# The first block of a fused two-layer matmul: w1 in row pieces, x turned in float16, six banks filled side by side

## The chip, the cores and the metric

The kernel runs on one core of a Trainium2 chip. A core has TensorE (PE, matrix products and transposes into PSUM, which has eight banks), VectorE (DVE), ScalarE (ACT), GpSimd (POOL) and SyncE (SP); ScalarE, GpSimd and SyncE also issue the transfers (DMAs) used here. The metric is the time of one execution on the device in microseconds; lower is better.

## The reference

`x` is 16 x 512 x 768, so 8192 rows of 768; `w1` is 768 x 3072, `w2` is 3072 x 768, all float32.

```python
y = np.matmul(x, w1) + b1
y = np.maximum(y, 0)
return np.matmul(y, w2).astype(np.float32)
```

## The kernel before

The rows are cut into eight blocks of 1024 (`MB`), the 3072 hidden columns into two halves, so there are 16 iterations (`NIT`); iterations 0 to 7 take the first half of the hidden columns, 8 to 15 the second and add to what is in the output. In each iteration a first stage computes `relu(x w1 + b1)` for its block and a second multiplies by `w2`. All products are float16 with float32 sums in PSUM. From iteration 1 on both stages use a scheme with fewer products, made of sums of tiles (`X_SUMS`, `W1_SUMS`, `Y_SUMS`, `W2_SUMS`) that VectorE adds up. The first stage of iteration 0 is different: `first_block` (L1008) multiplies plainly, since the sums of w1 aren't there yet.

The order of the work is a plan: every step is a task of a `Graph` with an engine, an assumed duration, what it reads and writes, and sometimes a due time. TensorE's tasks run in the order in which they are added; for the other engines `Graph.run` simulates the plan and picks among ready tasks by due time. It also gives out PSUM banks (`take`), by the times at which the plan believes them free. `presets` (L729) holds the times at which the plan believes the first transfers to have landed. The plan only fixes the order on each engine and the banks: on the chip each instruction waits for what it needs, and each engine runs its instructions in order.

What happens ahead of and in the first block:

- `prologue` (L708): SyncE and ScalarE issue two tiles each of x (128 rows, float32, into the slots `self.s[0..3]`), ScalarE then the bias rows (`load_bias`, L676). GpSimd issues the first strip of w1 (`load_strip`: 256 columns, all 768 rows, 384 KB once cast to float16), makes the constants, and then issues two more strips, the second half of x's block (`load_x`, cast to float16 into `self.xn[4..7]`), three strips of the second column group, `w2`, and the next block's x. TensorE multiplies a tile of ones eight times meanwhile.
- `add_transpose_first(half, s)` (L908): a tile of 128 rows of x is turned on TensorE in two pieces of three 128 x 128 squares, each piece in a bank of its own; VectorE copies the first piece to `self.x`, ScalarE the second. The first half of the block (four tiles, `half` 0) is turned in float32, the second in float16.
- `add_plain(strip, j, m, parts, evict_parts, between)`: the product of 128 hidden columns with 512 rows of half `m`; with `parts` 2 in two runs of six products of 256 rows. `between` is added after the first run. ScalarE then evicts the bank with bias and relu (L990) into `self.y`.
- `add_bias` (L938): the bias rows are turned on TensorE, VectorE copies them (L946) and builds tables from them (L949 to L961).

`first_block` adds the four turns of x, then strips 0, 1, 2 for half 0 (the bias turn after the first run of six products), with the turns of the second half's tiles put between runs, then the rest. Two steps that stand on VectorE and ScalarE in the same stretch matter below: the sums of w1 (L842) and squares of the weights for a later range check (L874).

Of the kernel before, what the change touches and what calls it, by code (L numbers as in the profile page):

```python
# [10 lines left out]
FP16 = mybir.dt.float16  # L11
# [3 lines left out]
ACTF = mybir.ActivationFunctionType  # L15
# [3 lines left out]
P = 128  # L19
# [567 lines left out]
class Fast:  # L587
# [93 lines left out]
    def load_strip(self, to, c, g, h):  # L681
# [4 lines left out]
            out=to[:, g, 2 * h:2 * h + 2].rearrange("p a k h -> p (a k) h"),  # L686
            in_=w1r[:, :, h0:h0 + 2 * P])

    def load_w2(self, to, c, h, q):
        h0 = (12 * c + 4 * h + q) * P  # L690
        self.nc.gpsimd.dma_start(out=to[:, 2 * q:2 * q + 2, h, :],
                                 in_=self.w2[h0:h0 + P, :].rearrange("p (a n) -> p a n", a=2))
# [15 lines left out]
    def prologue(self):  # L708
        nc = self.nc
        for s in range(4):  # L710
            (nc.sync, nc.scalar)[s % 2].dma_start(out=self.s[:, s],
                                                  in_=self.xf[s * P:(s + 1) * P, :])
        self.load_bias()
        self.load_strip(self.v1, 0, 0, 0)
        self.constants()
        self.load_strip(self.v1, 0, 0, 1)
        self.load_strip(self.v1, 0, 0, 2)
        self.load_x(0, 1, 2)
        for h in range(3):
            self.load_strip(self.v1, 0, 1, h)  # L720
        for q in range(4):
            for h in range(3):
                self.load_w2(self.v2, 0, h, q)
        self.load_x(1, 0)
        for _ in range(8):
            nc.tensor.matmul(self.ps[:, 7, 0:P], lhsT=self.ones, rhs=self.ones, start=True,
                             stop=True)

    def presets(self):  # L729
        g = self.g  # L730
        for t, at in enumerate((9.3, 11.3, 13.3, 19.9, 21.8, 23.8)):
            for k in range(2):
                g.preset(("w1", t // 3, 2 * (t % 3) + k), at)
        for q in range(4):
            for h in range(3):
                for n in range(2):
                    g.preset(("w2", 2 * q + n, h), 24.8 + 3 * q + h)
        for s in range(4):
            g.preset(("xn", 4 + s), 15.2 if s < 2 else 17.2)
            g.preset(("xn", s), 39.5)  # L740
            g.preset(("rows", s), (5.3, 5.3, 7.2, 7.2)[s])
        g.preset("b1_rows", 5.0)
# [162 lines left out]

    def add_transpose_first(self, half, s):  # L908

        for a in range(2):  # L910
            ps = Reg("ps", leaves=0)

            def view(ps=ps):
                p = self.ps[:, ps.at[0], :]
                if half:
                    p = p[:, 0:3 * P // 2].bitcast(FP16)
                return p[:, 0:3 * P].rearrange("p (k m) -> p k m", k=3)

            def turn(a=a, view=view):
                ident = (self.ident, self.ident16)[half]  # L920
                rows = self.xn[:, 4 + s, :] if half else self.s[:, s]
                for k in range(3):
                    self.nc.tensor.transpose(view()[:, k, :],
                                             rows[:, (3 * a + k) * P:(3 * a + k + 1) * P], ident)

            def copy(a=a, view=view):
                out = self.x_part(4 * half + s)[:, 3 * a:3 * a + 3]
                if a:
                    self.nc.scalar.copy(out=out, in_=view())
                else:  # L930
                    self.nc.vector.tensor_copy(out=out, in_=view())  # L931
            r = 2 * half + s // 2
            self.g.add("PE", 210 if half else 380, turn, writes=[ps],
                       reads=[("xn", 4 + s)] if half else [("rows", s), self.hold[s]])
            self.g.add("ACT" if a else "DVE", 560, copy, reads=[ps],
                       writes=[("x", 2 * r + a, s % 2)])

    def add_bias(self):  # L938
        nc = self.nc
# [29 lines left out]
    def add_plain(self, strip, j, m, parts, evict_parts, between=None):  # L969
        gi, h = divmod(strip, 3)  # L970
        ps = Reg("ps", leaves=2 if parts == 1 else 0)
        nc = self.nc

        def product(n):
            cols = slice(n * self.QM, (n + 1) * self.QM) if parts == 2 else slice(0, 512)
            for k2 in range(2):
                for k in range(3):
                    a = 4 * m + k2
                    rhs = (self.x[:, a:a + 3:2, k, :] if parts == 1
                           else self.x[:, a + 2 * n, k, :])  # L980
                    nc.tensor.matmul(self.ps[:, ps.at[0], cols],  # L981
                                     lhsT=self.v1[:, gi, 2 * h + k2, k, j * P:(j + 1) * P],
                                     rhs=rhs, start=(k2 == 0 and k == 0),
                                     stop=(k2 == 1 and k == 2))

        def evict(a, b):
            n = 4 * h + 2 * gi + j
            i = 8 * m + 2 * gi + j
            out = self.y[:, i:i + 5:4, h * self.QM:(h + 1) * self.QM]
            nc.scalar.activation(out=out[:, a:b],  # L990
                                 in_=self.ps[:, ps.at[0], :].rearrange("p (a m) -> p a m",
                                                                       a=2)[:, a:b],
                                 func=ACTF.Relu, bias=self.b1y[:, n:n + 1])
        for n in range(parts):
            rows = (0, 1) if parts == 1 else (n,)
            nc = self.nc
            self.g.add("PE", 1300 // parts, lambda n=n: product(n),
                       reads=[("x", 4 * m + 2 * r + k2, q) for r in rows for k2 in range(2)
                              for q in range(2)] + [("w1", gi, 2 * h + k) for k in range(2)],
                       writes=[ps])  # L1000
            if n == 0 and between:
                between()
        for a, b in ((0, 2),) if evict_parts == 1 else ((0, 1), (1, 2)):
            self.g.add("ACT", 692 if evict_parts == 1 else 470, lambda a=a, b=b: evict(a, b),
                       reads=[ps, "b1y"],
                       writes=[("y", (2 * m + r) * 4 + 2 * gi + j, h) for r in range(a, b)])

    def first_block(self):  # L1008
        for s in range(4):
            self.add_transpose_first(0, s)  # L1010
        plain = self.add_plain
        for strip in range(3):
            for j in range(2):
                between = None
                if strip == 0 and j == 0:
                    between = self.add_bias
                elif strip == 2 and j == 1:
                    between = lambda: [self.add_transpose_first(1, s) for s in (0, 1)]
                plain(strip, j, 0, 2, 2 if strip == 1 else 1, between)
        plain(0, 0, 1, 2, 1, lambda: [self.add_transpose_first(1, s) for s in (2, 3)])  # L1020
        plain(0, 1, 1, 2, 1)
        for strip in (1, 2):
            for j in range(2):
                plain(strip, j, 1, 2, 2 if strip == 1 else 1)
        for strip in (3, 4, 5):
            for m in range(2):
                for j in range(2):
                    plain(strip, j, m, 1, 1)
# [514 lines left out]
```

## Time and profile before

| | |
|---|---|
| median of 3 runs | 852.05 us (851.43 to 852.44) |
| profiled execution | 851.03 us, span 849.4 us |
| granted TensorE clock | 0.999 |
| busy: PE, DVE, ACT, POOL | 839.5, 736.5, 568.5, 166.5 us |
| first product of the first block (L981) | starts at 9.50 us |
| last TensorE row of the timeline | starts at 841.79 us, lasts 1.30 us |

The span is the time from the first to the last instruction; the profiled execution's own time is 1.6 us longer. A row of the timeline gives the start in us, the duration, engine, line and operation, the tile written and the tile read, how many instructions are merged in it, and in brackets how long the engine had been idle and what ended that. PEld is TensorE loading weights, which overlaps its products. A `q` behind an engine's name is its queue of transfers.

### The profile page before, as it was taken

How to read it: one execution, taken by the hardware profiler on the slowest of the kernel's cores; microseconds unless marked ns; L12 is line 12 of the kernel's file. 1: busy time of each engine (PE TensorE's matmuls, PEld its weight loads, DVE VectorE, ACT ScalarE, POOL GpSimd, SP SyncE). 2: the span in 40 equal slices, each digit the busy share in tenths (PEclk: the TensorE clock that was granted, in tenths of full speed). 3: DMA queues.
4: the chain of work that ended last, by engine and by line, in shares of the span. 5: the costliest groups of instructions: out<-in, count | busy, mean ns of one | idle time of the engine just before them, and what ended most of it. 6: DMA issues, size and time to landing. Idle time of an engine off the chain costs nothing.

```text
span 849.4 us, 16770 instructions
## 1 busy us (share of the span) xinstructions
PE 839.5 (99%) x6381; PEld 625.1 (74%) x6381; DVE 736.5 (87%) x1229; ACT 568.5 (67%) x1203; POOL 166.5 (20%) x181
## 2 busy tenths in 40 slices
PE   8999999999999999999999999999999999999997
PEld 7558778587786867768687686877868677686874
DVE  5898988969889697988999989698896979979787
ACT  5866967678686784946859477766657666456462
POOL 5210011102111020110031503224041230502301
PEclk9999999999999999999999999999999999999999
DMA  9996597969789496593894968979789797975937
GB/s 212 202 180 175 82 230 108 198 140 160 198 109 203 117 154 164 96 249 123 232 177 82 193 109 148 160 110 176 124 130 147 122 164 113 154 126 75 167 85 178
DMA packets 170968, 128.93 MB, mean 152 GB/s; under 512 B 93805, under 2 KB 169349, under 8 KB 170885
## 3 DMA queue, kind: packets, MB, share of 16 engines
q0 software_dynamic: 57104, 69.61, 53.3%
q1 hardware_dynamic: 113312, 57.23, 28.4%
q8 instruction: 50, 0.82, 0.4%
q10 hardware_dynamic: 468, 1.00, 0.3%
q14 instruction: 34, 0.27, 0.1%
HBM read 73.15 MB, written 69.60 MB: 168 GB/s over the span
## 4 chain that ended last, share of the span: by engine, by line


## 5 line engine op out<-in xcount | busy, mean ns | idle before, releaser
L1197 PE MATMUL ps<-v,y 128*128 128x384 f16 x2496 | 408.5, 326 | 0.5 <-ACT s L1208 0.5
L1071 PE MATMUL ps<-x,v 128*128 128x256 f16 x3600 | 395.6, 273 | 0.0
L1071 PEld LDWEIGHTS <-v 128*128 128x128 f16 x3600 | 352.0, 98 | 42.5
L1197 PEld LDWEIGHTS <-y 128*128 128x128 f16 x2496 | 244.0, 98 | 160.9 <-issue 1.0
L1208 ACT ACTIVATE s<-ps 128x384 f32<-128x384 f32 (+1 forms) x244 | 153.8, 643 | 137.4 <-PE ps L1197 136.3
L1044 DVE TENSOR_TENSOR y<-y 128x768 f16<-128x768 f16 (+1 forms) x384 | 219.0, 618 | 2.5
L1114 DVE CUSTOM_DVE_ANT_0 y<-ps,s 128x512 f16<-128x512 f32 x240 | 155.7, 685 | 54.2 <-ACT s L1111 41.9
L1250 POOL DMA_DIRECT2D out_dram<-s x79 | 95.2, 1467 | 166.7 <-ACT s L1208 112.7
L1111 ACT ACTIVATE s<-ps,bt 128x256 f32<-128x256 f32 x180 | 75.1, 469 | 63.2 <-PE ps L1071 57.4
L826 DVE TENSOR_TENSOR x<-x 128x768 f16<-128x768 f16 (+1 forms) x210 | 113.8, 578 | 1.4
L706 POOL DMA_DIRECT2D xn<-in_x_dram x30 | 25.1, 838 | 258.4 <-ACT xn L766 153.8
L1111 ACT ACTIVATE y<-ps,bt 128x256 f16<-128x256 f32 x180 | 69.6, 486 | 7.7 <-PE ps L1071 7.7
L1214 DVE TENSOR_TENSOR s<-ps,s 128x768 f32<-128x768 f32 x74 | 70.5, 952 | 1.7 <-PE ps L1197 0.9
L1208 ACT ACTIVATE ps<-ps 128x384 f32<-128x384 f32 (+1 forms) x144 | 68.1, 512 | 5.0 <-PE ps L1197 3.2
L1214 DVE TENSOR_TENSOR s<-s,ps 128x768 f32<-128x768 f32 x60 | 57.0, 950 | 2.8 <-PE ps L1197 0.5
L766 ACT ACTIVATE xn<-xn 128x768 f16<-128x768 f16 x64 | 53.5, 837 | 1.2 <-DMA x<-xn 1.2
L1253 POOL DMA_DIRECT2D out_dram<-s x16 | 18.9, 1184 | 108.6 <-ACT s L1208 97.3
L1111 ACT ACTIVATE ps<-ps,bt 128x256 f32<-128x256 f32 x60 | 26.7, 445 | 19.2 <-PE ps L1071 18.2
L1107 ACT ACTIVATE ps<-ps 128x512 f32<-128x512 f32 x60 | 35.3, 588 | 3.6 <-DVE y L1114 3.5
L1122 DVE TENSOR_TENSOR s<-s,ps 128x512 f32<-128x512 f32 x30 | 20.6, 687 | 17.8 <-PE ps L1071 17.8
L981 PE MATMUL ps<-x,v 128*128 128x256 f16 (+1 forms) x216 | 32.0, 308 | 0.7 <-DVE x L931 0.7
L1117 DVE SCALAR_TENSOR_TENSOR s<-ps,bt,s 128x256 f32<-128x256 f32 x60 | 26.1, 476 | 4.4 <-PE ps L1071 4.4
(59 smaller groups left out, 302.6 us busy)
## 6 DMA issues: line engine op xcount, KB each, us to landing
out_dram<-s POOLq DMA_DIRECT2D x95, 384.0 KB, 7.6
out_dram<-s SPq DMA_DIRECT2D x69, 384.0 KB, 4.6
xn<-in_x_dram POOLq DMA_DIRECT2D x28, 768.0 KB, 9.2
v<-in_w_dram POOLq DMA_DIRECT2D x6, 384.0 KB, 10.6
v<-in_w_dram POOLq DMA_DIRECT2D x12, 192.0 KB, 9.0
w1d<-in_w_dram POOLq DMA_DIRECT2D x6, 384.0 KB, 6.8
w2d<-in_w_dram POOLq DMA_DIRECT2D x12, 192.0 KB, 5.4
v<-w1d SPq DMA_DIRECT2D x12, 192.0 KB, 4.2
```

The lines of the kernel that those rows point to most:

```text
L766: self.nc.scalar.activation(out=self.xn[:, s, :], in_=self.xn[:, s, :], func=ACTF.Square, accum_out=self.stat[:, self.stat_at["x"] + i:][: ...
L826: self.nc.vector.tensor_tensor(out=self.two(x, out), in0=self.two(x, in0), in1=self.two(x, in1), op=ALU.add if sign > 0 else ALU.subtract)
L981: nc.tensor.matmul(self.ps[:, ps.at[0], cols], lhsT=self.v1[:, gi, 2 * h + k2, k, j * P:(j + 1) * P], rhs=rhs, start=(k2 == 0 and k == 0), ...
L1044: self.nc.vector.tensor_tensor(out=self.two(self.y, out), in0=self.two(self.y, in0), in1=self.two(self.y, in1), op=ALU.add if sign > 0 els ...
L1071: nc.tensor.matmul(self.ps[:, at, j * self.QM:(j + 1) * self.QM], lhsT=self.v1[:, gi, self.w1s[c][gi][FIRST_V[p]], k, j * P:(j + 1) * P], ...
L1107: nc.scalar.activation(out=out, in_=ps, scale=float(a), func=func if kind == "out" else ACTF.Copy)
L1111: nc.scalar.activation(out=out[:, j], in_=ps[:, j], func=func, scale=float(a), bias=beta(j))
L1114: nc.vector._custom_dve(TENSOR_ADD_SAT, out=out, in0=ps, in1=s, s0=F_MAX, s1=0.0)
L1197: nc.tensor.matmul(self.ps[:, bank[ch].at[j], 0:NH], lhsT=self.y[:, ys[SECOND_U[p]], m0:m0 + P], rhs=self.v2[:, slot[SECOND_V[p]], h, :], ...
L1208: nc.scalar.activation(out=out, in_=ps, func=ACTF.Copy, scale=float(a))
L1214: engine.tensor_tensor(out=out, in0=in0, in1=in1, op=ALU.add if a == b else ALU.subtract)
L1250: nc.gpsimd.dma_start(out=rows, in_=out, accum_op=ALU.add)
```

## The change

The three strips of w1 of column group 0 are loaded as six pieces instead (`load_part`): piece k holds rows 128k to 128k+127 of all three strips, 192 KB in float16. The plan's table of landing times has the six pieces.

The first half's four tiles of x are first cast to float16 (`add_casts`, first half of each tile on VectorE, second on ScalarE, into unused slots of `self.y`), and turned in float16. A tile is now turned as one task of six squares into one bank; VectorE and ScalarE each copy half of that bank.

`first_rows` replaces strips 0 to 2 of half 0: six banks, one for each pair of strip and 128 columns, are filled side by side. For each piece k and each half n of the 512 rows, six products are added, one per bank, so that a bank is complete only with the last piece. The order is piece 0 for the first 256 rows, the turns of tiles 2 and 3, piece 1 for the first 256 rows, pieces 0 and 1 for the second, and then pieces 2 to 5 for both; the turns of the second half's tiles stand before piece 5 and after it. The six evictions (`add_evict`, moved out of `add_plain`) come at the end.

The bias turn (`add_bias`) is now added right after the casts, ahead of all turns of x; before, it came after the first six products.

```diff
+    def load_part(self, g, k):
+        w1r = self.w1.rearrange("(k p) (h c) -> p k h c", p=P, c=4 * P)
+        self.nc.gpsimd.dma_start(out=self.v1[:, g, k // 3:6:2, k % 3, :],
+                                 in_=w1r[:, k, 0:3, 2 * g * P:2 * (g + 1) * P])
...
-        self.load_strip(self.v1, 0, 0, 0)
+        self.load_part(0, 0)
         self.constants()
-        self.load_strip(self.v1, 0, 0, 1)
-        self.load_strip(self.v1, 0, 0, 2)
+        for k in range(1, 6):
+            self.load_part(0, k)
...
+    def add_casts(self):
+        for s in range(4):
+            for a in range(2):
...
+                    out, rows = self.y[:, 16 + s, cols], self.s[:, s, cols]
+                    if a:
+                        self.nc.scalar.copy(out=out, in_=rows)
+                    else:
+                        self.nc.vector.tensor_copy(out=out, in_=rows)
...
+    def add_transpose_first(self, half, rows):
+        for s in rows:
             ps = Reg("ps", leaves=0)
...
+                tile = self.xn[:, 4 + s, :] if half else self.y[:, 16 + s, :]
+                for k in range(6):
+                    self.nc.tensor.transpose(view(k // 3)[:, k % 3, :],
+                                             tile[:, k * P:(k + 1) * P], self.ident16)
...
+            for a in range(2):
+                self.g.add("ACT" if a else "DVE", 480, lambda a=a, copy=copy: copy(a), reads=[ps],
+                           writes=[("x", 2 * r + a, s % 2)])
...
+    def first_rows(self):
+        banks = {(h, j): Reg("ps", leaves=0) for h in range(3) for j in range(2)}
...
+        for k, n in ((0, 0), (1, 0), (0, 1), (1, 1), *((k, n) for k in range(2, 6) for n in range(2))):
+            for h, j in banks:
+                self.g.add("PE", 109, lambda k=k, n=n, h=h, j=j: product(k, n, h, j),
+                           reads=[("x", 2 * n + k // 3, q) for q in range(2)] + [("part", k)],
+                           writes=[banks[h, j]])
+            if (k, n) == (0, 0):
+                self.add_transpose_first(0, (2, 3))
+            elif (k, n) == (4, 1):
+                self.add_transpose_first(1, (0, 1))
+        self.add_transpose_first(1, (2, 3))
+        for h, j in banks:
+            self.add_evict(h, j, 0, banks[h, j], 1)
...
     def first_block(self):
-        for s in range(4):
-            self.add_transpose_first(0, s)
...
+        self.add_casts()
+        self.add_bias()
+        self.add_transpose_first(0, (0, 1))
+        self.first_rows()
+        for j in range(2):
+            plain(0, j, 1, 2, 1)
```

The plan's entry for the bias rows stays as it was, `g.preset("b1_rows", 5.0)`.

More of the change, by code (lines that the diff above doesn't have):

```diff
@@ L730, in presets @@
         g = self.g
-        for t, at in enumerate((9.3, 11.3, 13.3, 19.9, 21.8, 23.8)):
+        parts = (8.2, 9.2, 10.2, 11.2, 12.3, 13.4)
+        for k in range(6):
+            g.preset(("part", k), parts[k])
+        for h, at in enumerate((19.9, 21.8, 23.8)):
             for k in range(2):
-                g.preset(("w1", t // 3, 2 * (t % 3) + k), at)
+                g.preset(("w1", 0, 2 * h + k), parts[3 * k + 2])
+                g.preset(("w1", 1, 2 * h + k), at)
         for q in range(4):
@@ L904, in add_stats, with cast @@
             add()
-    def add_transpose_first(self, half, s):
-        for a in range(2):
-            ps = Reg("ps", leaves=0)
[L913 to L926, printed above, removed]
+    def add_casts(self):
+        for s in range(4):
+            for a in range(2):
+                cols = slice(3 * a * P, 3 * (a + 1) * P)
+                def cast(s=s, cols=cols, a=a):
+                    out, rows = self.y[:, 16 + s, cols], self.s[:, s, cols]
[3 more added lines that the diff above has]
+                        self.nc.vector.tensor_copy(out=out, in_=rows)
+                self.g.add("ACT" if a else "DVE", 560 if a else 500, cast,
+                           reads=[("rows", s), self.hold[s]], writes=[("cast", s, a)], due=0.0)
@@ new lines, in add_transpose_first, with view, turn, copy @@
+    def add_transpose_first(self, half, rows):
+        for s in rows:
+            ps = Reg("ps", leaves=0)
+            def view(a, ps=ps):
+                p = self.ps[:, ps.at[0], 0:3 * P].bitcast(FP16)[:, 3 * a * P:3 * (a + 1) * P]
+                return p.rearrange("p (k m) -> p k m", k=3)
+            def turn(s=s, view=view):
+                tile = self.xn[:, 4 + s, :] if half else self.y[:, 16 + s, :]
+                for k in range(6):
+                    self.nc.tensor.transpose(view(k // 3)[:, k % 3, :],
+                                             tile[:, k * P:(k + 1) * P], self.ident16)
+            def copy(a, s=s, view=view):
@@ L927, in copy @@
                 out = self.x_part(4 * half + s)[:, 3 * a:3 * a + 3]
                 if a:
-                    self.nc.scalar.copy(out=out, in_=view())
+                    self.nc.scalar.copy(out=out, in_=view(a))
                 else:
-                    self.nc.vector.tensor_copy(out=out, in_=view())
+                    self.nc.vector.tensor_copy(out=out, in_=view(a))
             r = 2 * half + s // 2
-            self.g.add("PE", 210 if half else 380, turn, writes=[ps],
-                       reads=[("xn", 4 + s)] if half else [("rows", s), self.hold[s]])
@@ L935, in add_transpose_first @@
-            self.g.add("ACT" if a else "DVE", 560, copy, reads=[ps],
-                       writes=[("x", 2 * r + a, s % 2)])
+            self.g.add("PE", 420, turn, writes=[ps],
+                       reads=[("xn", 4 + s)] if half else [("cast", s, a) for a in range(2)])
+            for a in range(2):
+                self.g.add("ACT" if a else "DVE", 480, lambda a=a, copy=copy: copy(a), reads=[ps],
+                           writes=[("x", 2 * r + a, s % 2)])
     def add_bias(self):
@@ L984, in product @@
                                      stop=(k2 == 1 and k == 2))
[L986 to L993, printed above, removed]
         for n in range(parts):
@@ L1002, in add_plain, with add_evict, evict @@
                 between()
+        self.add_evict(strip, j, m, ps, evict_parts)
+    def add_evict(self, strip, j, m, ps, evict_parts):
+        gi, h = divmod(strip, 3)
+        nc = self.nc
+        def evict(a, b):
+            n = 4 * h + 2 * gi + j
+            i = 8 * m + 2 * gi + j
+            out = self.y[:, i:i + 5:4, h * self.QM:(h + 1) * self.QM]
+            nc.scalar.activation(out=out[:, a:b],
+                                 in_=self.ps[:, ps.at[0], :].rearrange("p (a m) -> p a m",
+                                                                       a=2)[:, a:b],
+                                 func=ACTF.Relu, bias=self.b1y[:, n:n + 1])
         for a, b in ((0, 2),) if evict_parts == 1 else ((0, 1), (1, 2)):
@@ L1006, in add_plain, with product @@
                        writes=[("y", (2 * m + r) * 4 + 2 * gi + j, h) for r in range(a, b)])
+    def first_rows(self):
+        nc = self.nc
+        banks = {(h, j): Reg("ps", leaves=0) for h in range(3) for j in range(2)}
+        def product(k, n, h, j):
+            nc.tensor.matmul(self.ps[:, banks[h, j].at[0], n * self.QM:(n + 1) * self.QM],
+                             lhsT=self.v1[:, 0, 2 * h + k // 3, k % 3, j * P:(j + 1) * P],
+                             rhs=self.x[:, 2 * n + k // 3, k % 3, :],
+                             start=(n == 0 and k == 0), stop=(k == 5), skip_group_check=True)
+        for k, n in ((0, 0), (1, 0), (0, 1), (1, 1), *((k, n) for k in range(2, 6) for n in range(2))):
[10 more added lines that the diff above has]
+            self.add_evict(h, j, 0, banks[h, j], 1)
     def first_block(self):
-        for s in range(4):
-            self.add_transpose_first(0, s)
         plain = self.add_plain
[L1012 to L1021, printed above, removed]
+        self.add_casts()
[4 more added lines that the diff above has]
+            plain(0, j, 1, 2, 1)
         for strip in (1, 2):
```

## The prediction

> **What bounds the kernel now.** I read the page first, then the order of time of TensorE in the first 24 us, then, for the same stretch, the queues, the groups by shape and the order of time of VectorE. The page:
>
> ```profile
> span 849.4 us, 16770 instructions
> PE 839.5 (99%) x6381; PEld 625.1 (74%) x6381; DVE 736.5 (87%) x1229; ACT 568.5 (67%) x1203; POOL 166.5 (20%) x181
> ...
> L1197 PE MATMUL ps<-v,y 128*128 128x384 f16 x2496 | 408.5, 326 | 0.5 <-ACT s L1208 0.5
> ...
> L981 PE MATMUL ps<-x,v 128*128 128x256 f16 (+1 forms) x216 | 32.0, 308 | 0.7 <-DVE x L931 0.7
> ```
>
> TensorE is busy for 839.5 of 849.4 us, so about 10 us can be won at all, and the two large groups hardly wait (L1197 idles 0.5 us). The built instruction streams of the two kernels agree on TensorE from the end of the first block on (11,677 instructions in the same order), so what the change does to the time is how much earlier or later TensorE leaves the first block. TensorE there:
>
> ```profile
> 1.29 3.78 PE L726 MATMUL ps<-ones 128*128 128x128 f32 x16 [1.29 <-DVE ones L666]
> 5.66 1.50 PE L923 MATMUL ps<-ident,s 128*128 128x128 f32 x12 [0.59 <-DMA s<-in_x_dram]
> 7.68 1.50 PE L923 MATMUL ps<-ident,s 128*128 128x128 f32 x12 [0.52 <-DMA s<-in_x_dram]
> 9.50 0.82 PE L981 MATMUL ps<-x,v 128*128 128x256 f16 x6 [0.32 <-DVE x L931]
> 10.24 0.24 PE L943 MATMUL ps<-ident,b_rows 24*128 24x24 f32 x1
> 10.41 6.72 PE L981 MATMUL ps<-x,v 128*128 128x256 f16 x60
> 16.97 0.83 PE L923 MATMUL ps<-ident,xn 128*128 128x128 f16 x12
> 17.64 1.59 PE L981 MATMUL ps<-x,v 128*128 128x256 f16 x12
> 19.07 0.83 PE L923 MATMUL ps<-ident,xn 128*128 128x128 f16 x12
> 20.26 3.98 PE L981 MATMUL ps<-x,v 128*128 128x256 f16 x35 [0.35 <-DVE x L931]
> ```
>
> The first product starts at 9.50, and the 79th (6+60+12 are before it) at 20.26, after one wait of 0.35. A product takes (16.97-10.41)/60 = 0.109 us, also across banks, a turn of a float16 piece (17.64-16.97)/12 = 0.056. What sets 9.50 is the first strip of w1, and strips then land 2.0 us apart, as the transfers queued behind them show:
>
> ```profile
> 1.87 0.65 ACTq L679 DMA_DIRECT2D b_rows<-in_b_dram  x1
> 9.39 0.64 PEld L981 LDWEIGHTS <-v 128*128 128x128 f16 x6 [0.46 <-DMA v<-in_w_dram]
> 11.63 0.71 POOL L691 DMA_DIRECT2D v<-in_w_dram  x1 [1.30 <-DMA v<-in_w_dram]
> 13.63 0.70 POOL L691 DMA_DIRECT2D v<-in_w_dram  x1 [1.29 <-DMA v<-in_w_dram]
> ```
>
> **The change part by part.**
>
> Pieces of w1. Half a strip takes half of 2.0 us, so the first piece lands about 1.0 us before 9.39, at 8.4, the others 1.0 us apart up to 13.4. GpSimd issues six transfers for three: five more at 0.70 us (L691 moves the same 192 KB) after its constants end later than the strips' issues did, but the queue is bound by data, so no landing moves. A step of twelve products takes 1.31 us, longer than the 1.0 us between pieces: later pieces are never waited for. Alone, this part is worth at most 1.0 us.
>
> Turns in float16. 24 float32 turns (2 x 1.50 us) go from the stretch before 9.50 and 24 float16 turns at 0.056 come. They stood beside the wait for w1, so nothing is won on the path; what is new is casts ahead and copies behind. A cast of float32 from SBUF isn't in the trace. The groups by shape (first two lines: the first 12 us; the others: 12 to 24 us; after the bar busy us and mean ns of one, then idle time ahead) have these neighbours:
>
> ```profile
> L931 DVE CAST x<-ps 128x384 f16<-128x384 f32 x4 | 2.2, 557 | 6.0 <-PE ps L923 5.8
> L929 ACT CAST x<-ps 128x384 f16<-128x384 f32 x4 | 1.9, 478 | 3.9 <-PE ps L923 3.9
> L929 ACT COPY x<-ps 128x384 f16<-128x384 f16 x4 | 1.7, 482 | 0.7 <-PE ps L923 0.7
> L931 DVE COPY x<-ps 128x384 f16<-128x384 f16 x4 | 1.3, 352 | 0.3 <-PE ps L923 0.3
> L842 DVE TENSOR_TENSOR v<-v 128x768 f16<-128x768 f16 x13 | 6.9, 554 | 3.6 <-DMA v<-in_w_dram 3.4
> L990 ACT ACTIVATE y<-ps,b1y 128x512 f16<-128x512 f32 x5 | 3.4, 687 | 2.1 <-PE ps L981 1.9
> ```
>
> On VectorE it lies between 0.35 (float16 copy) and 0.56 (cast out of PSUM), on ScalarE near 0.48. I take the upper ends; both ends give the same sum, because tiles 0 and 1 (there at 5.66) are cast by 6.8 and nothing uses them before 7.8, as follows.
>
> The bias. This is the step that decides. In the changed order on TensorE the turn of the bias rows stands ahead of all turns of x, and TensorE works in order. In the trace it stood at 10.24 and waited for nothing, so when its rows land isn't shown directly. Their transfer is the third on ScalarE's queue, behind two tiles of x (issued at 1.87). The queue tables from 6.2 to 7.2 us (first line) and from 7.2 to 9.5 us (second line, the only queue left) say when that queue, q10, ran dry:
>
> ```profile
> q10 hardware_dynamic: 57, 0.04, 12.2%
> ...
> q0 software_dynamic: 902, 0.45, 145.4%
> ```
>
> q10 still moves 57 packets after 6.2 and none after 7.2. The last x tile, whose packets end in the same stretch, released TensorE at 7.68. So the bias rows land between 6.5 (0.3 us after the earliest of those packets) and 7.75; I take 7.7, since they are last on the queue. From there it is a chain with nothing beside it, with VectorE's rows of before for its pieces:
>
> ```profile
> 10.52 0.18 DVE L946 COPY b1y<-ps 128x24 f32<-128x24 f32 x1 [1.07 <-PE ps L943]
> 10.74 0.24 DVE L957 TENSOR_SCALAR bt<-b1y 128x8 f32<-128x8 f32 x2
> 11.01 0.17 DVE L961 TENSOR_TENSOR bt<-bt,b1y 128x8 f32<-128x8 f32 x1
> 11.10 0.30 DVE L957 TENSOR_SCALAR bt<-b1y 128x8 f32<-128x8 f32 x3
> ...
> 12.24 0.55 DVE L842 TENSOR_TENSOR v<-v 128x768 f16<-128x768 f16 x1
> 13.36 4.21 DVE L842 TENSOR_TENSOR v<-v 128x768 f16<-128x768 f16 x8 [0.56 <-DMA v<-in_w_dram]
> 17.49 0.61 DVE L931 COPY x<-ps 128x384 f16<-128x384 f16 x2
> 17.51 0.86 ACT L929 COPY x<-ps 128x384 f16<-128x384 f16 x2 [0.30 <-PE ps L923]
> ```
>
> Bias turn at 7.8; its copy 0.28 later (10.24 to 10.52), 8.08; four small operations on bias tables stand ahead of the copies of x on VectorE, 0.65 from the copy's start (10.52 to 11.17, after the first of the three at 11.10), 8.73. VectorE copies its halves of tiles 0 and 1 from 8.73 and 8.99 (two take 0.61). Both halves of a tile now lie in one bank, and in the built streams ScalarE's copy waits for VectorE's of the same bank: from 9.1 and 9.48 (two take 0.86), so done at 9.96. The first product reuses the bank of tile 1 and waits for that last copy: 10.0, though its weights have been there since 8.4. Before, it was 9.50: the gain of 1.0 is gone, and 0.5 is lost.
>
> From the first product on. Six products (0.66), turns of tiles 2 and 3 (0.67, casts done by 10.4 on VectorE and 10.8 on ScalarE, each just in time), then 66 products and 24 turns; at the first product on tile 2 VectorE is behind (two casts, nine bias operations in 1.07 us, two copies, to about 12.1), for which I give 0.1. The turns of the second half's first tiles come at 10.0+0.66+0.67+0.1+54 x 0.109 = 17.3, product 73 at 17.3+0.67+12 x 0.109+0.67 = 19.95, product 79 at 20.6 if nothing waits: 0.35 later than 20.26.
>
> The end of the block. Product 79 needs the second half's last copies. ScalarE's copy of the first of these tiles starts 0.54 after its turn (16.97 to 17.51), 17.85, and ends at 18.33; VectorE waits for it (one bank again) and copies at 18.36 and 18.75, to 19.0. Then three sums of w1 stand ahead of its next copies: 8 take 4.21, three 1.4 to 1.65. The next two copies end at 21.05 to 21.25. So product 79 starts at about 21.1: a wait of 0.5. ScalarE's last copy follows VectorE's, 21.1+0.48 = 21.6, while product 82 is due at 21.43: 0.2. Six banks fill together now, and their evictions (0.69 each, about 0.6 apart) are interrupted by those copies: the third after them ends near 23.4, and product 97, due at 23.25, needs its bank: 0.15.
>
> The sum: 0.35+0.5+0.25+0.15 = 1.25, call it 1.3 us later, against the execution profiled: span 849.4, time 851.03, so 1.6 around the span. The median shown is 852.05, 1.0 above that execution; on it the sum gives 853.35. After the block nothing gives it back: the only idle time left there is the 0.5 us of L1197.
>
> **The clock.** Weight loads of one shape ran at two speeds:
>
> ```profile
> L726 PEld LDWEIGHTS ps<-ones 128*128 128x128 f32 x16 | 3.5, 330 | 1.3 <-DVE ones L666 1.3
> L923 PEld LDWEIGHTS ps<-ident,s 128*128 128x128 f32 x24 | 2.6, 140 | 1.6 <-issue 0.9 <-DVE x L931 0.7
> ```
>
> 330 ns in the warming products from 1.29 to 5.07, 140 ns from 5.66 on. Before, TensorE then rests for no more than 0.6 us at a time. In the changed kernel it works from 5.07 to 10.0 for only 0.8 us (bias and twelve turns), with a rest of 2.7 us ahead and one of 1.3 us behind. The Trainium skill, page "TensorE: Matmul & The Clock Gate", section Part 1, says that the clock falls to half after an idle window of about 3.4 us, and its section on oscillation tells to leave no gap over that. By that rule 2.7 us is just short and the sum stays; if a window with 0.8 us of work in it counts as idle too, it is the next rival.
>
> **The rivals.** The clock falls in that gap. For it: the sparse 4.9 us. Against: no rest is as long as the 3.8 us that the slow stretch lasted at the start. Price: products at half speed for a stretch like the first, 3.8 us, lose 1.9 us: 855.25. It decides as soon as more than 0.4 us of products run slow, for then the change is over 0.2% (1.7 us; about what a measurement of this kernel can tell from no change) slower.
>
> The bias rows land early. The plan's own table says 5.0. Then the first product starts with its weights at 8.5, 1.5 us earlier than in my sum, and what is left is 1.3-1.5 = -0.2: 851.85. Even then the waits at the end of the block (0.9) eat most of the gain. They would have to land before 6.4 for no loss; the queue's rows speak against it.
>
> The pieces land no earlier than a strip, at 9.4: TensorE isn't ready before 10.0, so the time stays at 853.35. That part of the change is hidden either way.
>
> VectorE gets through its three sums in time, or they stand elsewhere: 0.5+0.2 less, 852.65.
>
> **How the numbers follow.** My sum, with the last two rivals within it, 0.64: handoffs that I rounded (some twelve at 0.05) leave it between 852.6 and 854.2, and a third of that is over 853.75. The clock 0.26. The bias early 0.07. Something unlisted 0.03. Slower by over 0.2%: 0.22+0.26+0.02 = 0.50. Within: 0.42+0.05 = 0.47. Faster: 0.03, since even the best case ends at -0.2 us. The likeliest time is 853.35; the range runs from 852.1, just above the early bias, to 856.0, a little beyond the clock's 855.25.
>
> **What would show it.** Right: the bias turn is TensorE's first work after 5.07 and starts near 7.8, released by a DMA; the first product starts at about 10.0, released by ScalarE's copy; weights never end a wait; VectorE ends a wait of about 0.5 near 21.1. Wrong: first product at 8.5; products at 0.218 apiece after 10.0; no wait at the end of the block; TensorE stalling after 30 us where it did not before.

## The result, and the profile after

The changed kernel takes 854.4 us in the median (853.17 to 855.08), the kernel before 850.9 (850.52 to 852.84; the median of 852.05 shown ahead lies in the upper part of that). The ratio is 1.0035, 95% interval 1.0028 to 1.0042: slower, by some 3.0 us by the ratio and 3.5 between the medians. The granted clock of its 13 executions runs from 0.994 to 1.000, with 0.999 in the shortest (853.17) and 1.000 in the longest (855.08); what follows is read from one profiled execution of each kernel. That of the changed kernel took 854.89 us, with a granted clock of 0.995. From its page, the span, the busy times and the large group of products:

```profile
span 853.3 us, 16767 instructions
PE 840.4 (98%) x6381; PEld 626.2 (73%) x6381; DVE 737.4 (86%) x1233; ACT 569.2 (67%) x1205; POOL 168.6 (20%) x184
...
L1243 PE MATMUL ps<-v,y 128*128 128x384 f16 x2496 | 408.4, 326 | 0.5 <-ACT s L1254 0.5
```

The span grew by 3.9 us, TensorE's busy time by 0.9, and the second stage's products are as before (326 ns each, 0.5 idle). The order of time of TensorE shows where the rest lies:

```profile
1.29 3.63 PE L732 MATMUL ps<-ones 128*128 128x128 f32 x16 [1.29 <-DVE ones L666]
8.04 0.27 PE L966 MATMUL ps<-ident,b_rows 24*128 24x24 f32 x1 [3.12 <-DMA b_rows<-in_b_dram]
8.24 1.46 PE L945 MATMUL ps<-ident,y 128*128 128x128 f16 x12
10.66 1.44 PE L1043 MATMUL ps<-x,v 128*128 128x256 f16 x6 [0.96 <-ACT x L951]
...
19.90 0.83 PE L945 MATMUL ps<-ident,xn 128*128 128x128 f16 x12
...
22.55 0.82 PE L1004 MATMUL ps<-x,v 128*128 128x256 f16 x6
23.67 2.42 PE L1004 MATMUL ps<-x,v 128*128 128x256 f16 x18 [0.30 <-DVE x L953]
```

TensorE waits 3.12 us for the bias rows, then 0.96 for ScalarE's copy of x, and product 79 starts at 23.67 instead of 20.26. Products a little later (about 22 us in the profile of before) are 3.82 late; that is nearly all of the 3.9. But twelve turns take 1.46 at 8.24 and 0.83 at 19.90: TensorE ran at half speed for a while. Stretches cut at the changes of the granted clock (columns: busy us of TensorE and its instructions, granted clock, DMA share, GB/s):

```profile
4.63:8.04 3.41, 0.29 (x4) 1.00 1.17 309
8.04:11.45 3.41, 2.45 (x17) 0.50 1.43 191
11.45:14.87 3.42, 3.42 (x24) 0.50 1.29 205
14.87:18.28 3.41, 3.41 (x33) 1.00 1.29 201
```

Between 4.63 and 8.04 TensorE worked 0.29 us; then the clock was half for 6.83 us, twice 3.41. (Ahead of the first change that a trace records, this column reads 1.00 also where products run slow, as in the warming at the start.) The same stretches of the kernel before, whose clock had risen at 5.31 and stayed up:

```profile
5.31:8.72 3.41, 2.54 (x22) 1.00 1.28 275
8.72:12.13 3.41, 3.09 (x28) 1.00 1.45 197
```

VectorE and then ScalarE in the changed kernel, around the bias:

```profile
8.34 0.18 DVE L969 COPY b1y<-ps 128x24 f32<-128x24 f32 x1 [2.01 <-PE ps L966]
...
9.09 0.36 DVE L953 COPY x<-ps 128x384 f16<-128x384 f16 x1
9.73 0.36 DVE L953 COPY x<-ps 128x384 f16<-128x384 f16 x1 [0.28 <-PE ps L945]
```

```profile
9.49 0.48 ACT L951 COPY x<-ps 128x384 f16<-128x384 f16 x1 [3.04 <-DVE x L953]
10.12 0.48 ACT L951 COPY x<-ps 128x384 f16<-128x384 f16 x1 [0.16 <-DVE x L953]
```

The chain is the forecast one: bias turn, its copy, bias tables, VectorE's copy, ScalarE's copy of the same bank, first product. The second tile's copies wait 0.28 for the turns besides, which run at half speed.

### The profile page after: what moved, and what is told of

Same layout as the page of the kernel before. It is cut to its first block, busy times and chain, and to the rows that moved or that the text cites. A ratio compares the mean times of both kernels' runs of the same rounds, so it can differ in the third digit from the quotient of the medians.

```text
span 853.3 us, 16767 instructions
## 1 busy us (share of the span) xinstructions
PE 840.4 (98%) x6381; PEld 626.2 (73%) x6381; DVE 737.4 (86%) x1233; ACT 569.2 (67%) x1205; POOL 168.6 (20%) x184
## 4 chain that ended last, share of the span: by engine, by line
## 5 line engine op out<-in xcount | busy, mean ns | idle before, releaser
L1153 ACT ACTIVATE y<-ps 128x512 f16<-128x512 f32 x30 | 17.9, 596 | 16.7 <-PE ps L1117 16.7
```

What stands on the lines that cost most here:

```text
L1153: nc.scalar.activation(out=out, in_=ps, scale=float(a), func=func if kind == "out" else ACTF.Copy)
```

## The experiments

Two theories stood against each other. By the first, the order costs the time: the bias turn ahead of x, with the waits behind it. By the second, the order only leaves TensorE so little to do that the clock falls, and half speed costs the larger part. The letters in the expectations are others: theory A there takes both costs together, and B, C, D and the rivals are told where they come. Each edit is given against the changed kernel, or against the kernel before where that is said. Fences show the order of time, and the stretches of the granted clock with the columns as above. Shifts "in the block" below compare the start of the same product at about 22 us with that in the profile of before.

### Enough work for the clock, all else as changed (e2_warm)

```diff
-        for _ in range(8):
+        for _ in range(15):
             nc.tensor.matmul(self.ps[:, 7, 0:P], lhsT=self.ones, rhs=self.ones, ...
```

> The changed kernel with 15 products of ones at the start instead of 8, so that TensorE works until about 6.5 us; nothing else is changed and the bias turn still waits for its rows. Theory A: the clock stays full after 8 us (products 0.109 apart from the first on), first product still at 10.0 to 10.2, a wait of 0.3 to 0.5 near the end of the block, time 852.0 to 852.5: of the 3.5 us lost, 2 to 2.4 were the clock and 1.2 to 1.3 the bias and the waits. Theory B (the clock only fell in the one execution that was profiled): time as the changed kernel's, 854.4.

Ratio to before 1.0019 (1.0010 to 1.0028), median 852.45 us. TensorE's order of time, and the stretch of 3.41 us that holds most of the gap:

```profile
7.94 0.21 PE L966 MATMUL ps<-ident,b_rows 24*128 24x24 f32 x1 [0.28 <-DMA b_rows<-in_b_dram]
...
10.14 0.81 PE L1043 MATMUL ps<-x,v 128*128 128x256 f16 x6 [1.21 <-ACT x L951]
...
20.06 0.82 PE L1004 MATMUL ps<-x,v 128*128 128x256 f16 x6
21.19 5.04 PE L1004 MATMUL ps<-x,v 128*128 128x256 f16 x41 [0.31 <-DVE x L953]
```

```profile
7.11:10.52 3.41, 1.92 (x22) 1.00 1.42 190
```

The clock stays up, and the block is 1.34 late: the order with its waits is worth 1.34, and 3.82-1.34 = 2.48 go to half speed. Both theories hold, the clock with the larger part. The median moved less than 2.48 (854.4-852.45 = 1.95), because in this kernel a later wait, at 155 us, is 0.56 longer; it comes up again below.

### The bias turn later (e1_bias_late)

```diff
             if (k, n) == (0, 0):
+                self.add_bias()
                 self.add_transpose_first(0, (2, 3))
...
         self.add_casts()
-        self.add_bias()
         self.add_transpose_first(0, (0, 1))
```

> The changed kernel with one step moved: the bias turn stands behind the first six products, as before the change, instead of ahead of all turns of x. Theory A (two costs: the bias rows hold TensorE until about 8.0 us, and the long rest ahead of them lets its clock fall): first product at 8.5 to 8.7, longest rest of TensorE between 5 and 10 us under 1.8 us, clock full from the first turn on, time 850.5 to 851.2, about that of the kernel before, because the waits at the end of the block (0.9 us in sum) stay. Theory B (the six banks and the copies behind them cost most, the bias little): still 853 or more.

Ratio 1.0007 (0.9998 to 1.0016), median 851.58 us; block 0.77 late.

```profile
5.94 0.96 PE L945 MATMUL ps<-ident,y 128*128 128x128 f16 x12 [0.93 <-DVE y L929]
8.39 1.46 PE L1043 MATMUL ps<-x,v 128*128 128x256 f16 x6 [1.49 <-DMA v<-in_w_dram]
9.78 0.30 PE L966 MATMUL ps<-ident,b_rows 24*128 24x24 f32 x1
```

```profile
4.82:8.23 3.41, 1.15 (x14) 1.00 1.21 308
8.23:11.64 3.41, 3.25 (x21) 0.50 1.39 186
```

The first piece of w1 is there at 8.39, and TensorE takes it at once. Yet the clock still falls, after a stretch with 1.15 us of work and no rest above 1.49 us, here for one 3.41 alone. No rest of the length of the stretch is needed: little work in it is enough. The six banks and the copies behind them are all still here, so they are not what costs most (theory B).

### The bias rows issued first (e3_bias_dma_first)

```diff
+        self.load_bias()
         for s in range(4):
...
-        self.load_bias()
         self.load_part(0, 0)
```

> The changed kernel with the bias rows' transfer issued first on ScalarE's queue instead of third; all orders of instructions on the engines are those of the changed kernel. Theory A: the bias rows are there before the first x tile, the bias turn runs before 6 us and holds nothing; ScalarE's two x tiles come up to 0.65 us later; first product at 8.5 to 8.9; clock full; time 850.5 to 851.3. Theory B: 853 or more, as the order on the engines is the changed kernel's own.

Ratio 1.0011 (1.0003 to 1.0020), median 852.15 us; block 1.48 late.

```profile
5.00 0.25 PE L966 MATMUL ps<-ident,b_rows 24*128 24x24 f32 x1
...
8.88 1.46 PE L1043 MATMUL ps<-x,v 128*128 128x256 f16 x6 [1.66 <-DMA v<-in_w_dram]
```

```profile
8.48:11.89 3.41, 3.01 (x21) 0.50 1.42 188
```

Ahead of x on its queue the bias rows are there by 5.00: it was their place on the queue that held TensorE. The first product comes 1.78 earlier than in the changed kernel, but the clock falls at 8.48 all the same.

### The same order put into the kernel before (e4_before_bias_first)

```diff
     def first_block(self):
+        self.add_bias()
...
-                if strip == 0 and j == 0:
-                    between = self.add_bias
-                elif strip == 2 and j == 1:
+                if strip == 2 and j == 1:
```

> The kernel before with this one part of the change: its bias turn ahead of all turns of x. Theory A: TensorE rests from 5.1 to 7.9, then bias and 24 float32 turns (2.6 us); first product at 10.6 to 10.9 instead of 9.50; with a full clock 851.9 to 852.3, and if the clock falls in the rest of 2.8 us, up to 854. Theory B: within 0.5 us of the kernel before, 850.9.

Ratio 1.0033 (1.0020 to 1.0046), median 853.88 us; block 3.06 late.

```profile
8.09 0.27 PE L943 MATMUL ps<-ident,b_rows 24*128 24x24 f32 x1 [3.31 <-DMA b_rows<-in_b_dram]
8.29 4.23 PE L923 MATMUL ps<-ident,s 128*128 128x128 f32 x24
12.84 7.37 PE L981 MATMUL ps<-x,v 128*128 128x256 f16 x66 [0.32 <-DVE x L931]
```

```profile
7.76:11.17 3.41, 3.08 (x15) 0.50 1.45 197
```

Moving the bias turn, without pieces, casts or float16, costs 3.06 of the 3.82 us: a wait of 3.31 us, and half speed after it.

### Float16 turns alone (e8_before_f16)

```diff
     def first_block(self):
+        self.add_casts()
...
-                ident = (self.ident, self.ident16)[half]
-                rows = self.xn[:, 4 + s, :] if half else self.s[:, s]
+                ident = self.ident16
+                rows = self.xn[:, 4 + s, :] if half else self.y[:, 16 + s, :]
```

> The kernel before with this one part of the change: its first four x tiles cast to float16 and turned in float16 (two banks a tile, bias where it was, w1 in strips). Theory A: first product still at 9.5, since it waits for w1; but the turns take 1.7 us instead of 3.0, TensorE is busy for only about a third of 3.4 us there, the clock falls and products run at half speed until about 11.5: 851.5 to 852.5. Rival (only the rest of 2.8 us behind the bias makes the clock fall): 850.6 to 851.2.

Ratio 1.0021 (1.0011 to 1.0030), median 852.41 us; block 0.84 late.

```profile
9.33 1.46 PE L995 MATMUL ps<-x,v 128*128 128x256 f16 x6
10.72 0.30 PE L957 MATMUL ps<-ident,b_rows 24*128 24x24 f32 x1
```

```profile
4.92:8.34 3.42, 1.32 (x18) 1.00 1.23 300
8.34:11.75 3.41, 3.39 (x22) 0.50 1.45 196
```

The first product starts 0.17 earlier than before, but the clock has fallen at 8.34, under the turns ahead of it, and its six take 1.46 instead of 0.82. That the turns took longer in float32 cost nothing on the path, but they were the 2.54 us of work that held the clock.

### Bias late, and longer warming or filling (e5_late_warm, e7_late_fill)

The first is the edit of e1 with that of e2. The second is the edit of e1 with five products of ones in a free bank between the first turns and the first product:

```diff
+    def add_fill(self, n):
+        ps = Reg("ps", leaves=0)
+
+        def fill():
+            for _ in range(n):
+                self.nc.tensor.matmul(self.ps[:, ps.at[0], 0:P], lhsT=self.ones, rhs=self.ones,
+                                      start=True, stop=True)
+        self.g.add("PE", 220 * n, fill, writes=[ps])
...
         self.add_transpose_first(0, (0, 1))
+        self.add_fill(5)
         self.first_rows()
```

> The changed kernel with both of the earlier edits: the bias turn behind the first six products and 15 products of ones at the start. Theory A (bias order and clock are separate costs, the rest of the change gains up to 1.2 us): clock full from the first product on, first product between 8.5 and 9.4 (the longer start may hold the turns of x), time 849.6 to 850.4, under the kernel before. Theory C (the waits at the end of the block cancel the gain): 850.7 to 851.1, level with the kernel before.

> The changed kernel with the bias turn behind the first six products and five products of ones between the turns of tiles 0 and 1 and the first product (8 at the start as before). Theory A: TensorE is busy for over half of every stretch of 3.4 us from 1.3 us on, the clock stays full, first product at 8.4 to 8.6, time 849.4 to 850.0. Theory C: 850.7 to 851.1.

Longer warming: 1.0005 (0.9996 to 1.0014), median 851.36; block 0.27 late. Its clock stays up, but TensorE now reaches the second half's x before it has landed:

```profile
16.85 0.84 PE L945 MATMUL ps<-ident,xn 128*128 128x128 f16 x12 [0.51 <-DMA xn<-in_x_dram]
```

Filling: 1.0000 (0.9991 to 1.0009), median 850.71; block 0.28 earlier than before.

```profile
8.64 0.83 PE L1052 MATMUL ps<-x,v 128*128 128x256 f16 x6 [0.24 <-ACT y L927]
9.40 0.24 PE L966 MATMUL ps<-ident,b_rows 24*128 24x24 f32 x1
```

```profile
4.77:8.19 3.42, 2.02 (x24) 1.00 1.19 312
```

With 2.02 us of work in the gap the clock holds. Against e1 that is 0.77+0.28 = 1.05 us, although the first product starts 0.25 later here (x came later too: the casts start at 5.79, in e1 at 5.52); one stretch at half speed costs at least that here. So the rest of the change, freed of the bias and the clock, is worth 0.28 in the block. It does not last: at 39.19 TensorE waits for an eviction of ScalarE, and from there to 155 us the kernel is 0.07 late. The median is one that theory C had forecast.

### Longer warming in the kernel before (e6_before_warm)

The edit of e2 in the kernel before.

> The kernel before with 15 products of ones at the start instead of 8. Theory A: its turns of x keep the clock already, so nothing is gained: 850.6 to 851.2, first product at 9.5, clock full in both. Rival (the kernel before also loses time to the clock in some executions): under 850.4.

Ratio 1.0019 (1.0010 to 1.0028), median 852.43 us, though its block is 0.10 earlier. What is longer is one wait of the second stage at 155 us that ScalarE ends. It is the 0.5 of L1197 in the page of before. TensorE there, before and with the longer warming:

```profile
155.53 2.27 PE L1197 MATMUL ps<-v,y 128*128 128x384 f16 x13 [0.49 <-ACT s L1208]
```

```profile
156.58 1.14 PE L1197 MATMUL ps<-v,y 128*128 128x384 f16 x6 [1.64 <-ACT s L1208]
```

In that place ScalarE, in order, stands at the square of a tile of x whose transfer is late, with evictions behind it:

```profile
155.22 0.84 ACT L766 ACTIVATE xn<-xn 128x768 f16<-128x768 f16 x1 [2.36 <-DMA x<-xn]
156.06 0.85 ACT L1208 ACTIVATE s<-ps 128x384 f32<-128x384 f32 x2
```

The wait is 1.15 longer than before's. With -0.10 that is 1.05 of the 1.57 by which the medians differ; its profiled span is only 0.8 longer, so the rest lies between executions and isn't explained. Since this wait changes from kernel to kernel, medians of kernels with another start differ by more than their blocks do, and the sizes here are taken from the blocks.

### The square without its late transfer (e10_before_warm_junk, e12_before_junk, e11_best)

The square's output goes to a scratch tile, so that it no longer overwrites its input: in the kernel of e6, in the kernel before, and in that of e9 (told next).

```diff
-            self.nc.scalar.activation(out=self.xn[:, s, :], in_=self.xn[:, s, :],
+            self.nc.scalar.activation(out=self.junk, in_=self.xn[:, s, :],
...
-        self.g.add("ACT", 930, square, writes=[("xn", s), ("stat", "x", i)], due=due, idle=True)
+        self.g.add("ACT", 930, square, reads=[("xn", s)], writes=["junk", ("stat", "x", i)],
+                   due=due, idle=True)
```

> The kernel before with 15 products at the start, and ScalarE's squares of x (for the range check) written to a scratch tile instead of over x itself, so that they need not wait until x has been turned by the transfers; the plan then places them elsewhere. Theory D (the 1.5 us that 15 products cost the kernel before are the wait at 155 us, where evictions queue on ScalarE behind such a square): no wait over 0.2 us of TensorE near 155 us, time 850.0 to 850.9. Rival (the longer start costs by itself): 852 or more.

> The kernel before with only the squares of x written to the scratch tile. Theory D: the wait of 0.65 us at 155 us is gone and nothing else changes, 850.1 to 850.5. Rival: 850.7 to 851.1, since the plan moves the squares to places where others wait.

> The late bias turn, the five filling products and whole-tile copies in the second half, together with the squares written to a scratch tile. Theory A and D together: 0.5 to 0.7 us at the block and 0.6 us at 155 us, 849.4 to 850.0, faster than both kernels. Rival (the squares' new places make other waits): 850.6 or more.

1.0035 (1.0022 to 1.0047), 1.0031 (1.0020 to 1.0041) and 1.0036 (1.0024 to 1.0049): all three slower. The wait at 155 us is gone, but the plan orders VectorE and ScalarE otherwise, and new waits come instead. From the lists of TensorE's waits (us in total, times, longest), the longest new one of the kernel made from e6 and of the one made from e9:

```profile
PE ps L1072 <- ACT y L1108: 0.9, 1, 0.9
```

```profile
PE ps L1265 <- DVE s L1282: 1.9, 1, 1.9
```

In the profiled execution of e12, though, 1.51 of the 2.0 us by which its span is longer are there in the first block, which its edit leaves alone; the last section comes back to it. So the runs don't settle how much of the 1.57 of e6 that wait explains.

### Filling, and whole copies in the second half (e9_fill_whole)

On e7; in the second half each tile is copied by one engine, so that no copy waits for the other engine's.

```diff
+            if half:
+                def whole(s=s, ps=ps):
+                    p = self.ps[:, ps.at[0], 0:3 * P].bitcast(FP16)
+                    p = p.rearrange("p (k m) -> p k m", k=6)
+                    if s < 2:
+                        self.nc.scalar.copy(out=self.x_part(4 + s), in_=p)
+                    else:
+                        self.nc.vector.tensor_copy(out=self.x_part(4 + s), in_=p)
+                self.g.add("ACT" if s < 2 else "DVE", 840 if s < 2 else 660, whole, reads=[ps],
+                           writes=[("x", 2 * r + a, s % 2) for a in range(2)])
+                continue
```

> As the kernel with the late bias turn and five filling products, but in the second half of the block one engine copies a whole turned tile (ScalarE tiles 0 and 1, VectorE tiles 2 and 3), so that no copy waits for another of the same bank, and VectorE's sums of w1 stand ahead of its copies while ScalarE is copying. Theory A (the shared banks and the three sums cost about 0.4 us at the end of the block once the clock is kept): TensorE 0.5 to 0.7 us ahead of the kernel before from 22 us on instead of 0.28; time 850.2 to 850.6. Rival: no less waiting, as the last copy moves behind the evictions: 850.7 or more.

Ratio 0.9991 (0.9982 to 1.0000), median 850.17 us: the best of all kernels here, though the interval touches no change.

```profile
18.89 0.82 PE L1015 MATMUL ps<-x,v 128*128 128x256 f16 x6
20.21 6.05 PE L1015 MATMUL ps<-x,v 128*128 128x256 f16 x54 [0.50 <-DVE x L964]
```

VectorE still comes late behind its sums (0.50), and product 79 starts at 20.21, only 0.05 ahead of before; the block is 0.05 early where that of e7 was 0.28 early, so the whole copies did not help it. Its span is 848.5, 0.9 shorter, and 0.65 of that is there after 155 us, where its TensorE has no wait: the gain is for the most part not that of the copies.

## Why the prediction was right or wrong

**Only the first block matters: held.** The block is 3.82 late, the span 3.9 longer, and no wait was added after it.

**The chain of the bias: held.** Bias turn 7.8 forecast (the rows by 7.75 at the latest), 8.04 measured; first product released by ScalarE's copy; VectorE's wait at product 79. With the clock up (e2) the whole sum comes out: first product 10.0 forecast and 10.14 measured, product 73 at 19.95 and 20.06, product 79 at 21.1 and 21.19. The wait of 0.5 there was 21.19-20.06-6 x 0.109 = 0.48; the row's 0.31 counts from the end of the last product drawn. The 0.4 behind it for ScalarE's copy and the evictions was 1.34-0.93 = 0.41. In all 1.34, where the sum had 1.25. (In it stand 0.25 for ScalarE's last copy, where its own times, 21.1+0.48 against 21.43, give 0.15.)

**The pieces: held.** First piece at 8.4 forecast, 8.39 seen in e1; weights end no wait in the changed kernel. So the rival that pieces land no earlier falls.

**The bias early: not tested with the clock up.** Its case was -0.2. The -0.28 of e7 comes near by other means, but VectorE ends no wait at product 79 there, so the nearness is in part chance. In e3, where the rows do come early, the first product starts at 8.88 where the rival had 8.5, the clock falls, and the block is 1.48 late.

**"Nothing is won" by float16 turns: wrong.** Forecast as worth nothing on the path, they cost 0.84 alone (e8). The cover that I named, the wait for w1, was real, but what the turns did there, keeping TensorE at work, wasn't in the sum.

**The clock: the step that failed.** The likeliest case left the clock up, because "no rest is as long as the 3.8 us that the slow stretch lasted". The rest was 3.12 and the clock fell; in e1 none was above 1.49 and it fell. The rival with 855.25 was the case that came; its 0.26 was too small and its price of 1.9 for one slow stretch too. It was 2.48: two stretches of 3.41, with 2.45+3.42 = 5.87 us of work in them; half of that is 2.9. Of the difference 0.25 lay beside the wait for ScalarE's copy (0.96, where e2 has 1.21); the rest isn't traced. The Trainium skill, page "TensorE: Matmul & The Clock Gate", section Part 1, tells of a fall after an idle window of about 3.4 us, and that this window runs freely. The traces agree on the length (3.41 between changes) and differ on "idle": 1.32 us of work in a window didn't keep the clock (e8).

**The number.** 853.35 was forecast from a median of 852.05 that the later runs of before put at 850.9. As a difference it is +1.3 forecast and +3.5 measured (+3.0 by the ratio). By luck the high median hid 1.15 of the 2.2 that the sum fell short. Between the two profiled executions it is 3.9, and most of what the sum lacks of these is the clock's 2.48. The time measured, 854.4, lies inside the range, 0.85 below the clock's rival; the range reached that far only for this rival's sake.

## What to carry to other kernels

Ask of every step that is taken from an early, loosely filled stretch what it did for the clock: here the slower float32 turns held it, and five products of ones in their place cost nothing on the path (in e9, with the same five, the weights end the wait for the first product, at 8.36). Work that needs a small load mustn't be put first on an engine that works in order while that load is last on its queue. Sum up TensorE's work in each 3.4 us of an order; its longest rest alone doesn't tell whether the clock stays.

## What was not expected of the hardware

- In these traces the clock goes by how much TensorE works in a window of 3.41 us, not by whether it works. It fell after windows with 0.29, 1.15 and 1.32 us of work, and held after ones with 1.92, 2.02 and 2.54. The windows in which TensorE ends its work narrow this: after 1.37 us (e11, from 844.89) it fell, after 1.43 (e2, from 843.37) it held for one more window.
- To come back it wants more than it needs to stay: after the half-speed window with 2.45 us of work (changed kernel) it stayed down for another, after 3.01 (e3), 3.08 (e4) and 3.25 (e1) it rose. The row below has 2.57 and no rise; where between 2.57 and 3.01 the bound lies is open.
- Where the windows begin differs from one profiled execution to the next: falls at 8.04, 8.23, 8.48, 7.76 and 8.34 us in five kernels whose TensorE starts alike. In the profiled execution of e12, whose start is that of before, the window from 3.12 held 2.57 us of work and wasn't enough, so the clock first rose at 9.95, and the unchanged block was 1.51 late. The granted clock of an execution doesn't count such a late rise, and how often it came in executions without a profile isn't shown; in e8 those with 0.999 (852.16 to 853.63 us) are no shorter than those with 0.997 (851.50 to 851.76). The window of e12:

```profile
3.12:6.54 3.42, 2.57 (x13) 1.00 0.98 368
```
